# Earlier zeros for the experts' rows, later router loads and preparation, in a hybrid attention and mixture-of-experts block

## The chip, the cores and the metric

The kernel runs on one core of a Trainium2 chip. The metric is the device time of one launch in microseconds. Five engines run side by side, each through its own list of instructions in a fixed order: PE (matrix multiply; its weight load is PEld), DVE (vector), ACT (scalar functions), POOL (a second vector engine) and SP, which here only issues transfers. ACT and POOL can issue transfers too; all of them run on the core's 16 DMA engines.

## The reference

One block over 512 tokens of width 1024, in fp32, cut here to what the change meets:

```
proj   = x @ w_in                              # many column groups
y_a    = gated_deltanet(conv+silu of q, k, v, gates a, b, z)
y_b    = nsa_attention(q, compressed / selected / window keys, values)
merged = sigmoid(gate)*y_a + sigmoid(gate)*y_b
h1     = layer_norm(a*x  + merged @ w_out)
h2     = layer_norm(a*h1 + attention(h1 @ wq, mem @ wkv) @ xa_wo)   # over the memory
p      = softmax(h2 @ w_group + b_group);  group = top 1 of 4
e      = 2 best of the group's 8 experts by softmax(h2 @ w_expert + b_expert)
ffn    = sum over chosen experts of wt * (silu(h2@w_gate) * (h2@w_up)) @ w_down
out    = layer_norm(a*h2 + ffn)
```

The router's two products share one pass: `wr` holds both weight matrices (40 columns). The kernel takes them on rows that are not yet normalised, so that the scale `ln2_g` is multiplied into `wr` beforehand, and two sums over the rows (`ws2`, with `ln2_g` and `ln2_b`) correct the result afterwards.

## The kernel before

**Precision.** Each large product is three matmuls: every operand is split into a high part (a copy by ACT, rounded, L138) and a low part (source minus high, on DVE or POOL, L139), and `mm3` adds high*high, high*low and low*high (L211, L212, L213). `load_w` (L144) loads 256 columns of a weight matrix by SP, 1 MB, and splits them at once; so each block of weights passes SP, ACT, DVE or POOL, and then PE.

**Order.** One Python generator, `Weave`, writes the program. `dense` yields the projection blocks one after the other with the next block's weights loaded ahead; `W.until("k01")` writes all blocks up to a label, and `W.chain(gen, label)` writes a chain of dependent steps and fills between them with that many microseconds of projection blocks. A scheduler then places the instructions of each engine by its own estimate; `tc.issue_after` pins what is in it behind a place. Each engine then runs its list strictly in order. Big tiles come from 21 buffers (`B8`), tiles of 128x512 from a ring of six (`t512`).

**The start.** Blocks z3, k00, k01 come first. `token_gates` (L357 to L385) computes the gates' decay `gg` by a chain of small DVE operations (L359 to L375), then two matmuls over it (L377, L378), and exponentials on ACT (L382, L381, L385); `rotary_sines` follows (L286, L287 on ACT, L288 to L290 on POOL). Each key head passes ACT L421, three DVE steps L424, ACT L427 and DVE L428 (convolution and silu), then is transposed by PE (L217) and squared by ACT (L460) into `sst`. When all four heads' sums of squares are there, `gdn_inverse(0)` starts on DVE with L480, and goes through ACT L499 (decay, from PE L496 and L497), DVE L505, a forward substitution on DVE (L534 and L535, 15 steps) and L542 to L547 to the first small matmuls at PE L554.

**The middle.** After the sparse attention (`nsa`), `merged_T` k=7 transposes and splits the last piece of `merged`, the input of `w_out` (`dense_ln`, L941 adds the residual). Then come the attention over the memory (L1086 to L1116), `xa_wo` by `dense_ln`, whose first 256 columns (j = 0) run in blocks of 128 tokens t = 0 to 3, the router (`raw`, `after`, `route`) and the 32 experts, whose rows are added by indirect writes (L1310) into `ybuf`, 4 MB in DRAM, that must hold zeros before. `clear_ybuf` writes these zeros: POOL sets one 128x512 tile to zero, and one DMA writes it 16 times over. It is called when the first block of the memory's projections, x0, is reached, by `mem_load`, between the loads of x1's weights and of the memory.

**The router's tiles.** `wr` and `rb` (weights and biases) and `gb`, `gbp` (`ln2_g`, `ln2_b` in two layouts) come by eight small DMAs from the ACT queue (L1155 to L1166), and DVE makes `ws2` from them (L1168, L1171). `router_sums` (L1176 to L1178) adds `ws2` over the partitions with one matmul and copies it back.

Of the kernel before, what the change touches and what calls it, by code (L numbers as in the profile page):

```python
# [27 lines left out]
OP = mybir.AluOpType  # L28
AX = mybir.AxisListType
# [4 lines left out]
KD = D // 128  # L34
# [50 lines left out]
def body(tc, I, O, dbg=None):  # L85
    nc = tc.nc
    ctx = ExitStack()
    with ctx:
        _body(ctx, tc, nc, I, O, dbg or {})


def _body(ctx, tc, nc, I, O, dbg):
    V, A, T, G = nc.vector, nc.scalar, nc.tensor, nc.gpsimd
# [12 lines left out]
    def dump(name, ap):  # L106
        if name in dbg:
            nc.sync.dma_start(dbg[name], ap)
# [12 lines left out]
    def B8(shape, dt=FT):  # L121
        return big.tile(shape, dt, name="b8", bufs=NB8)

    def t512(shape, dt=FT):
        return wk.tile(shape, dt, name="t512", bufs=6)
# [8 lines left out]
    def load_rows(dst, src):  # L134
        nc.sync.dma_start(dst, src.rearrange("(t p) d -> p t d", p=128))
# [98 lines left out]
    def to_T(dh, dl, src, n_tok_tiles):  # L234

        for k in range(KD):
            p = ps.tile([128, 512], FT, name="tp")
            for t in range(n_tok_tiles):
                T.transpose(p[:, t * 128:(t + 1) * 128], src(t, k), ident)
            n = n_tok_tiles * 128  # L240
            split(dh[k // 4][:, k % 4, :n], dl[k // 4][:, k % 4, :n], p[:, :n])
# [22 lines left out]
    def before(engine):  # L264

        return [i for i in nc.cur_bb.bb.instructions if i.engine == engine][-1]
# [17 lines left out]
    def rotary_sines():  # L284
        with tc.issue_after(before(mybir.EngineType.Activation)):
            A.activation(ropec, ropes, AF.Sin, scale=0.5)  # L286
            A.activation(ropes, ropes, AF.Sin)  # L287
        G.tensor_scalar(ropes, ropes, sgn, None, op0=OP.mult)  # L288
        G.tensor_tensor(ropec, ropec, ropec, op=OP.mult)
        G.tensor_scalar(ropec, ropec, -2.0, 1.0, op0=OP.mult, op1=OP.add)  # L290
        dump("ropec", ropec)
        dump("ropes", ropes)
# [4 lines left out]
    p = ps.tile([128, 512], FT, name="tp")  # L297
# [13 lines left out]
    def proj_ch(hi, lo, c, out):  # L311
        for k in range(KD):
# [6 lines left out]
                                     ap=[[0, 128], [1, 128]]))  # L319
# [660 lines left out]
    def clear_ybuf(eng):  # L980
        z = t512([128, 512])
        G.memset(z, 0.0)
        eng.dma_start(ybuf.rearrange("(p a) (b c) -> p (a b) c", p=128, b=2), z[:, None, :].to_broadcast([128, 16, 512]))
# [2 lines left out]
    ME = {}  # L986

    def mem_load():
        clear_ybuf(nc.sync)
        memh, meml = B8([128, KD, M], FR), B8([128, KD, M], FR)  # L990
        mn = B8([128, 2, D])
        load_rows(mn, I["mem"][0])
        to_T([memh[:, 0:4], memh[:, 4:8]], [meml[:, 0:4], meml[:, 4:8]],
             lambda t, k: mn[:, t, k * 128:(k + 1) * 128], 2)
        ME.update(h=memh, l=meml, k=B8([128, KD, M]), v=B8([128, 2, D]))

    def mem_block(j):
        def emit(hi, lo):
            if not ME:
                mem_load()  # L1000
            memh, meml = ME["h"], ME["l"]
            if j < 4:
                for c in range(2):
                    p = ps.tile([128, 512], FT, name="mm")
                    for k in range(KD):
                        yield 0.33
                        mm3(p[:, :M], hi[:, k, c * 128:(c + 1) * 128], lo[:, k, c * 128:(c + 1) * 128],
                            memh[:, k], meml[:, k], first=k == 0, last=k == KD - 1)
                    A.activation(ME["k"][:, 2 * j + c], p[:, :M], AF.Copy)
            else:  # L1010
                for t in range(2):
                    p = ps.tile([128, 512], FT, name="mm")
                    for k in range(KD):
                        yield 0.33
                        mm3(p[:, :256], memh[:, k, t * 128:(t + 1) * 128], meml[:, k, t * 128:(t + 1) * 128],
                            hi[:, k, :256], lo[:, k, :256], first=k == 0, last=k == KD - 1)
                    A.activation(ME["v"][:, t, 256 * (j - 4):256 * (j - 4) + 256], p[:, :256], AF.Copy)
        return ("x%d" % j, I["xa_wkv"][0], 256 * j, 256, emit)
# [25 lines left out]
    W.until("z3")  # L1044
    token_gates()
    rotary_sines()
    W.until("k01")
    W.chain(gdn_inverse(0), "k11")
    W.until("v01")
# [50 lines left out]
    for t in range(NT):  # L1100
        P = PP[t][:, 0].rearrange("p (a b) -> p a b", a=4)
        PT = PP[t][:, 1].rearrange("p (a b) -> p a b", a=8)
        for q in range(2):
            p = ps.tile([128, 512], FT, name="tp")
# [4 lines left out]
    for t in range(NT):  # L1109
        PT = PP[t][:, 1].rearrange("p (a b) -> p a b", a=8)  # L1110
        for q in range(2):
            po = ps.tile([128, 4, 128], FT, name="ga", bufs=4)
            for i in range(4):
                c = 4 * q + i
# [24 lines left out]
    def load_next(n):  # L1139
        for e, q in use[:n]:  # L1140
            WT[e, q] = load_gu(e, q) if q < 2 else load_down(e)
        del use[:n]

    early.close()
    late = ctx.enter_context(tc.tile_pool(name="late", bufs=1))
    identr = late.tile([128, 128], FR, name="identr")
# [5 lines left out]
    wr = late.tile([128, KD, 40], FT, name="wr")  # L1152
    wb = t512([128, KD, 40])
    V.memset(wr[:, :, 4:8], 0.0)
    nc.scalar.dma_start(wr[:, :, 0:4], I["moe_w_group"][0].rearrange("(k p) c -> p k c", p=128))  # L1155
    nc.scalar.dma_start(wr[:, :, 8:40], I["moe_w_expert"][0].rearrange("(k p) c -> p k c", p=128))
    rb = late.tile([128, 40], FT, name="rb")
    V.memset(rb[:, 4:8], NEG)
    for n, c0, c1 in (("moe_b_group", 0, 4), ("moe_b_expert", 8, 40)):
        nc.scalar.dma_start(rb[:, c0:c1], bass.AP(tensor=I[n].tensor, offset=I[n].offset, ap=[[0, 128], [1, c1 - c0]]))  # L1160

    gb = late.tile([128, 2, KD], FT, name="gb")
    gbp = late.tile([128, 2, KD], FT, name="gbp")
    for i, n in enumerate(("ln2_g", "ln2_b")):
        nc.scalar.dma_start(gb[:, i], I[n][0].rearrange("(k p) -> p k", p=128))
        nc.scalar.dma_start(gbp[:, i], I[n][0].rearrange("(p k) -> p k", k=KD))  # L1166
    for i, w_ in ((1, wb), (0, wr)):
        V.tensor_tensor(w_, wr, gb[:, i, :, None].to_broadcast([128, KD, 40]), op=OP.mult)  # L1168
    ws2 = late.tile([128, 2, 40], FT, name="ws2")
    for i, w_ in enumerate((wr, wb)):  # L1170
        V.tensor_reduce(ws2[:, i], w_.rearrange("p k c -> p c k"), axis=AX.X, op=OP.add)  # L1171

    def router_sums():
        p = ps.tile([128, 512], FT, name="tp")
# [425 lines left out]
    with tc.If(most > CAP):  # L1600
# [5 lines left out]
        for t in range(NT):  # L1606
            for q in range(2):
                p = ps.tile([128, 512], FT, name="tp")
# [54 lines left out]
```

## Time and profile before

| | us |
|---|---|
| median of 3 runs | 1255.44 (1253.97 to 1255.5) |
| profiled execution | 1254.66 |
| its span | 1252.9 |
| PE busy | 1161.7 (93%) |
| DVE busy | 658.2 (53%) |
| ACT busy | 459.3 (37%) |
| POOL busy | 181.9 (15%) |
| mean granted clock of PE | 0.969 |

The profile's times are microseconds from the start of the span. In a timeline a row gives the start, the duration, engine, line, operation, output<-input, and in brackets how long the engine had been idle and what released it. [...]

### The profile page before, as it was taken

What the parts mean: (1) busy time and instruction counts of PE and PEld (TensorE: products, weight loads), DVE (VectorE), ACT (ScalarE), POOL (GpSimd) and SP (SyncE); (2) the same over time, 40 slices, a digit from 0 to 9 for tenths busy, and PEclk for the clock granted to TensorE, in tenths of its full rate; (3) what the DMA queues carried; (4) which work ended last, traced back from release to release, by engine and by line L of the source; (5) the groups of instructions that cost most, each with busy time, mean ns of one, the idle gap of its engine ahead of it and who ended that gap; (6) DMA issues with size and microseconds to landing.
All of it is one profiled execution on the core that took longest, in us unless ns stands there. A gap on an engine that the chain in (4) does not pass through costs nothing. (4 is left out here: it accounts for less than half of the span.)

```text
span 1252.9 us, 20776 instructions
## 1 busy us (share of the span) xinstructions
PE 1161.7 (93%) x8356; PEld 925.4 (74%) x8356; DVE 658.2 (53%) x1657; ACT 459.3 (37%) x1093; POOL 181.9 (15%) x151
## 2 busy tenths in 40 slices
PE   6996998879999999999899899999989999999994
PEld 6885787758888879999798799789985455455532
DVE  4695477874775724556457758233484111111147
ACT  4643454534544214343345524334142111111224
POOL 4151221221000000000001102000020000000185
PEclk9998999989999999999899999999998999999997
DMA  8220212112142562212531343227546899999823
GB/s 268 68 68 3 68 34 69 34 35 69 39 131 69 173 212 69 69 35 67 187 93 58 122 120 101 68 67 255 204 145 248 302 384 380 407 392 379 338 77 133
DMA packets 101882, 189.22 MB, mean 151 GB/s; under 512 B 10246, under 2 KB 74438, under 8 KB 97680
## 3 DMA queue, kind: packets, MB, share of 16 engines
q1 hardware_dynamic: 93456, 181.58, 41.1%
q0 software_dynamic: 2224, 3.94, 1.0%
q10 hardware_dynamic: 6096, 2.27, 0.8%
q8 instruction: 68, 1.11, 0.4%
q14 instruction: 38, 0.31, 0.1%
HBM read 177.93 MB, written 13.63 MB: 153 GB/s over the span
## 5 line engine op out<-in xcount | busy, mean ns | idle before, releaser
L211 PE MATMUL mm<-b,b 128*128 128x256 f32 (+3 forms) x1216 | 404.2, 333 | 21.7 <-ACT b L138 7.2
L212 PE MATMUL mm<-b,b 128*128 128x256 f32 (+3 forms) x1216 | 392.2, 323 | 2.2 <-DVE b L139 2.2
L213 PE MATMUL mm<-b,b 128*128 128x256 f32 (+3 forms) x1216 | 391.5, 322 | 0.7 <-POOL b L139 0.4
L211 PEld LDWEIGHTS mm<-b,b 128*128 128x128 f32 x1216 | 233.1, 192 | 43.3 <-issue 17.1
L213 PEld LDWEIGHTS mm<-b,b 128*128 128x128 f32 x1216 | 233.1, 192 | 22.1 <-issue 3.8
L212 PEld LDWEIGHTS mm<-b,b 128*128 128x128 f32 x1216 | 233.7, 192 | 18.2 <-DVE b L139 2.8
L1447 PE MATMUL ga<-b,b 128*64 128x512 f32 x512 | 131.5, 608 | 6.8 <-DVE b L1334 6.8
L139 DVE TENSOR_TENSOR b<-b,b 128x2048 fp32r<-128x2048 f32 (+4 forms) x48 | 101.8, 2123 | 56.5 <-ACT b L138 48.0
L138 ACT ACTIVATE b<-b 128x2048 fp32r<-128x2048 f32 (+4 forms) x58 | 104.3, 1799 | 26.9 <-DMA b<-in_w_in_dram 7.4
L1447 PEld LDWEIGHTS ga<-b,b 128*64 128x64 f32 x512 | 38.4, 138 | 73.8 <-issue 64.1
L424 DVE SCALAR_TENSOR_TENSOR t<-mm,cw,t 128x511 f32<-128x511 f32 (+2 forms) x72 | 53.8, 747 | 32.3 <-ACT t L421 31.1
L217 PE MATMUL tp<-cs,b 128*128 128x128 f32 x376 | 59.4, 287 | 9.7 <-DMA cs<-in_cst_dram 5.9
L1462 PE MATMUL ga<-b,t 128*64 128x512 f32 x256 | 63.9, 593 | 0.5 <-ACT t L1306 0.5
L139 POOL TENSOR_TENSOR b<-b,b 128x2048 fp32r<-128x2048 f32 x10 | 45.9, 4593 | 123.2 <-ACT b L138 102.1
L1327 PE MATMUL mm<-t,b 128*128 128x256 f32 x240 | 61.5, 294 | 0.0
L1299 DVE SCALAR_TENSOR_TENSOR t<-t,ga 128x256 f32<-128x256 f32 x16 | 6.7, 420 | 98.2 <-ACT t L1298 98.1
L217 PEld LDWEIGHTS tp<-cs,b 128*128 128x128 f32 x376 | 45.4, 147 | 15.3 <-DMA cs<-in_cst_dram 5.9
L1327 PEld LDWEIGHTS mm<-t,b 128*128 128x128 f32 x240 | 48.8, 203 | 0.8 <-issue 0.8
L1462 PEld LDWEIGHTS ga<-b,t 128*64 128x64 f32 x256 | 20.0, 137 | 36.2 <-issue 35.1
L815 POOL MEMSET b<- 128x97 f32 x32 | 5.6, 179 | 272.6 <-PE ga L762 170.7
L1310 POOL DMA_INDIRECT ybuf<-b,idx x14 | 13.7, 980 | 215.4 <-ACT b L1470 111.2
L1306 ACT ACTIVATE t<-tp 128x256 f32<-128x256 f32 x16 | 6.1, 383 | 88.8 <-PE tp L217 88.8
(442 smaller groups left out, 1842.4 us busy)
## 6 DMA issues: line engine op xcount, KB each, us to landing
b<-in_moe_w_gate_dram SPq DMA_DIRECT2D x64, 512.0 KB, 10.3
b<-in_moe_w_up_dram SPq DMA_DIRECT2D x64, 512.0 KB, 10.7
b<-in_moe_w_down_dram SPq DMA_DIRECT2D x32, 1024.0 KB, 12.6
b<-in_w_in_dram SPq DMA_DIRECT2D x22, 1024.0 KB, 5.3
b<-in_w_in_dram SPq DMA_DIRECT2D x10, 1040.0 KB, 5.2
b<-in_cmp_w_dram SPq DMA_DIRECT2D x16, 512.0 KB, 8.4
b<-in_xa_wkv_dram SPq DMA_DIRECT2D x8, 1024.0 KB, 5.3
ybuf<-t SPq DMA_DIRECT2D x1, 4096.0 KB
```

The source lines that it names most:

```text
L138: A.activation(hi, src, AF.Copy)
L139: eng.tensor_tensor(lo, src, hi.bitcast(FT), op=OP.subtract)
L211: T.matmul(out, wh, xh, start=first, stop=False)
L212: T.matmul(out, wh, xl, start=False, stop=False)
L213: T.matmul(out, wl, xh, start=False, stop=last)
L217: T.transpose(dst_psum[:, i * 128:(i + 1) * 128], s_, ident)
L424: V.scalar_tensor_tensor(acc[:, s_:], pp[:, :S - s_], cw[:, c_:c_ + 1], acc[:, s_:], op0=OP.mult, op1=OP.add)
L1299: V.scalar_tensor_tensor(th, th, 1.0, ph[:, :256], op0=OP.add, op1=OP.mult)
L1310: G.indirect_dma_start(out=ybuf[:, :], out_offset=bass.IndirectOffsetOnAxis(ap=idx, axis=0), in_=yt, in_offset=None, bounds_check=2 * S - ...
L1327: T.matmul(p, rows_of(hl)(t)[:, c], sv, start=False, stop=t == NT - 1)
L1447: T.matmul(ph[64 * i:64 * i + 64], xg[:, k, 128 * pp + 64 * i:128 * pp + 64 * i + 64], WT[2 * pr + i, k // 4][:, :, k % 4], start=k == 0, ...
L1462: T.matmul(py[64 * i:64 * i + 64], hT[:, k, 64 * i:64 * i + 64], WT[2 * pr + i, 2][:, k, 512 * n:512 * n + 512], start=k == 0, stop=k == 1)
```

## The change

The zeros are written right after `rotary_sines`, by the ACT queue, instead of in `mem_load` by SP. The router's eight DMAs go from the ACT queue to SP's, pinned behind the SP instructions that stood there when the attention over the memory was written; the four DVE operations that make `ws2` are pinned behind DVE's.

```
--- before.py
+++ after.py
@@ -986,7 +986,6 @@
     ME = {}
 
     def mem_load():
-        clear_ybuf(nc.sync)
         memh, meml = B8([128, KD, M], FR), B8([128, KD, M], FR)
         mn = B8([128, 2, D])
         load_rows(mn, I["mem"][0])
@@ -1044,6 +1043,7 @@
     W.until("z3")
     token_gates()
     rotary_sines()
+    clear_ybuf(nc.scalar)
     W.until("k01")
     W.chain(gdn_inverse(0), "k11")
     W.until("v01")
@@ -1141,6 +1141,7 @@
             WT[e, q] = load_gu(e, q) if q < 2 else load_down(e)
         del use[:n]
 
+    behind_attention = [before(e) for e in (mybir.EngineType.SP, mybir.EngineType.DVE)]
     early.close()
     late = ctx.enter_context(tc.tile_pool(name="late", bufs=1))
     identr = late.tile([128, 128], FR, name="identr")
@@ -1152,23 +1153,26 @@
     wr = late.tile([128, KD, 40], FT, name="wr")
     wb = t512([128, KD, 40])
     V.memset(wr[:, :, 4:8], 0.0)
-    nc.scalar.dma_start(wr[:, :, 0:4], I["moe_w_group"][0].rearrange("(k p) c -> p k c", p=128))
-    nc.scalar.dma_start(wr[:, :, 8:40], I["moe_w_expert"][0].rearrange("(k p) c -> p k c", p=128))
     rb = late.tile([128, 40], FT, name="rb")
     V.memset(rb[:, 4:8], NEG)
-    for n, c0, c1 in (("moe_b_group", 0, 4), ("moe_b_expert", 8, 40)):
-        nc.scalar.dma_start(rb[:, c0:c1], bass.AP(tensor=I[n].tensor, offset=I[n].offset, ap=[[0, 128], [1, c1 - c0]]))
 
     gb = late.tile([128, 2, KD], FT, name="gb")
     gbp = late.tile([128, 2, KD], FT, name="gbp")
-    for i, n in enumerate(("ln2_g", "ln2_b")):
-        nc.scalar.dma_start(gb[:, i], I[n][0].rearrange("(k p) -> p k", p=128))
-        nc.scalar.dma_start(gbp[:, i], I[n][0].rearrange("(p k) -> p k", k=KD))
-    for i, w_ in ((1, wb), (0, wr)):
-        V.tensor_tensor(w_, wr, gb[:, i, :, None].to_broadcast([128, KD, 40]), op=OP.mult)
     ws2 = late.tile([128, 2, 40], FT, name="ws2")
-    for i, w_ in enumerate((wr, wb)):
-        V.tensor_reduce(ws2[:, i], w_.rearrange("p k c -> p c k"), axis=AX.X, op=OP.add)
+    with tc.issue_after(behind_attention[0]):
+        for i, n in enumerate(("ln2_g", "ln2_b")):
+            nc.sync.dma_start(gb[:, i], I[n][0].rearrange("(k p) -> p k", p=128))
+        nc.sync.dma_start(wr[:, :, 0:4], I["moe_w_group"][0].rearrange("(k p) c -> p k c", p=128))
+        nc.sync.dma_start(wr[:, :, 8:40], I["moe_w_expert"][0].rearrange("(k p) c -> p k c", p=128))
+        for n, c0, c1 in (("moe_b_group", 0, 4), ("moe_b_expert", 8, 40)):
+            nc.sync.dma_start(rb[:, c0:c1], bass.AP(tensor=I[n].tensor, offset=I[n].offset, ap=[[0, 128], [1, c1 - c0]]))
+        for i, n in enumerate(("ln2_g", "ln2_b")):
+            nc.sync.dma_start(gbp[:, i], I[n][0].rearrange("(p k) -> p k", k=KD))
+    with tc.issue_after(behind_attention[1]):
+        for i, w_ in ((1, wb), (0, wr)):
+            V.tensor_tensor(w_, wr, gb[:, i, :, None].to_broadcast([128, KD, 40]), op=OP.mult)
+        for i, w_ in enumerate((wr, wb)):
+            V.tensor_reduce(ws2[:, i], w_.rearrange("p k c -> p c k"), axis=AX.X, op=OP.add)
 
     def router_sums():
         p = ps.tile([128, 512], FT, name="tp")
```

Since the scheduler places every instruction anew, the order also moves where the diff says nothing. Names as `t_455` are tiles; behind the new tile of the zeros their numbers are higher by three.

On DVE, at the start: `t_408` (after: `t_411`) and `t_455` (after: `t_458`) are the first and the second key head of k00; `gg` is the end of the gate chain. Before:

```order
L424 SCALAR_TENSOR_TENSOR t_408<-mm,cw,t_408 128x509
L371 TENSOR_TENSOR gp<-gp,gu 128x32
L372 TENSOR_SCALAR gp<-gp 128x32
L373 TENSOR_TENSOR gp<-gp,gs 128x32
L374 SCALAR_TENSOR_TENSOR gp<-gx,gp 128x32
L428 SCALAR_TENSOR_TENSOR b_381<-t_413,t_408 128x512
L375 SCALAR_TENSOR_TENSOR gg<-gp,ea 128x32
L379 COPY gcum<-tp 128x32
L380 TENSOR_SCALAR gcn<-tp 128x32
L383 TENSOR_SCALAR egn<-egc 128x32
L384 TENSOR_TENSOR ekd<-gcn,tp 128x32
L424 SCALAR_TENSOR_TENSOR t_455<-mm,cw,t_455 128x511
```

After:

```order
L424 SCALAR_TENSOR_TENSOR t_458<-mm,cw,t_458 128x510
L371 TENSOR_TENSOR gp<-gp,gu 128x32
L424 SCALAR_TENSOR_TENSOR t_458<-mm,cw,t_458 128x509
L372 TENSOR_SCALAR gp<-gp 128x32
L371 TENSOR_TENSOR gp<-gp,gu 128x32
L372 TENSOR_SCALAR gp<-gp 128x32
L371 TENSOR_TENSOR gp<-gp,gu 128x32
L428 SCALAR_TENSOR_TENSOR b_384<-t_463,t_458 128x512
L372 TENSOR_SCALAR gp<-gp 128x32
L373 TENSOR_TENSOR gp<-gp,gs 128x32
L374 SCALAR_TENSOR_TENSOR gp<-gx,gp 128x32
L375 SCALAR_TENSOR_TENSOR gg<-gp,ea 128x32
```

The gate chain's end, L375, stood ahead of the second head's three L424; now it stands behind them and behind that head's L428, which waits for ACT's L427.

On ACT, from there to the third key head's silu (`t_508` and `t_513`, after: `t_511` and `t_516`). Before:

```order
L421 ACTIVATE t_455<-mm,cw 128x512
L138 ACTIVATE b_479<-b_477 128x8x256
L427 ACT_TABLE_LOAD
L427 ACTIVATE t_460<-t_455 128x512
L421 ACTIVATE t_508<-mm,cw 128x512
L499 ACTIVATE b_599<-ga,gcn 128x128 x4
L458 ACTIVATE b_382<-tp 128x512
L460 ACTIVATE sq,sst<-tp 128x128 x4
L427 ACTIVATE t_513<-t_508 128x512
L421 ACTIVATE t_555<-mm,cw 128x512
```

After:

```order
L458 ACTIVATE b_385<-tp 128x512
L460 ACTIVATE sq,sst<-tp 128x128 x4
L138 ACTIVATE b_482<-b_480 128x8x256
L421 ACTIVATE t_511<-mm,cw 128x512
L499 ACT_TABLE_LOAD
L499 ACTIVATE b_602<-ga,gcn 128x128 x8
L427 ACTIVATE t_516<-t_511 128x512
L421 ACTIVATE t_558<-mm,cw 128x512
L458 ACTIVATE b_385<-tp 128x512
L460 ACTIVATE sq,sst<-tp 128x128 x4
L427 ACTIVATE t_563<-t_558 128x512
```

Eight of the L499, which wait for PE, now stand ahead of the third head's L427; four stood behind the third head's L421.

On ACT, at the last split of `merged` (`b_6847`) and the split of the second block of `w_out` (`b_7340`). Before:

```order
L138 ACTIVATE b_6847<-tp 128x512
L854 ACTIVATE sq<-mm,a_7260 128x128
L1155 DMA wr<-in_moe_w_group_dram 128x8x4
L1156 DMA wr<-in_moe_w_expert_dram 128x8x32
L1160 DMA rb<-in_moe_b_group_dram 128x4
L1160 DMA rb<-in_moe_b_expert_dram 128x32
L138 ACTIVATE b_6847<-tp 128x512
L138 ACTIVATE b_7340<-b_7338 128x8x256
```

After:

```order
L899 DMA b_7335<-in_ln_b_dram 128x1024
L138 ACTIVATE b_6847<-tp 128x512
L854 ACTIVATE sq<-mm,a_7260 128x128
L138 ACTIVATE b_6847<-tp 128x512
L138 ACTIVATE b_7340<-b_7338 128x8x256
L138 ACTIVATE b_7450<-b_7448 128x8x256
L138 ACTIVATE b_7560<-b_7558 128x8x256
```

The four DMA issues that stood between the two splits of `b_6847` are gone, and so are the four behind `b_7340`.

On ACT, at the first blocks of `xa_wo`: `b_8388` and `b_8389` are the splits of the attention's output, `b_8699` the split of the second 256 columns' weights, `ws` the router's sums. Before:

```order
L138 ACTIVATE b_8388<-ga 128x512 x2
L1177 ACTIVATE ws_8664<-tp 128x80
L1017 ACTIVATE b_6371<-mm 128x256 x2
L138 ACTIVATE b_8388<-ga 128x512 x2
L138 ACTIVATE b_8389<-ga 128x512 x4
L138 ACTIVATE b_8699<-b_8697 128x8x256
L138 ACTIVATE b_8809<-b_8807 128x8x256
```

After:

```order
L138 ACTIVATE b_8388<-ga 128x512 x2
L1016 ACTIVATE b_6371<-mm 128x256 x2
L138 ACTIVATE b_8388<-ga 128x512 x2
L138 ACTIVATE b_8389<-ga 128x512 x4
L1181 ACTIVATE ws_8654<-tp 128x80
L138 ACTIVATE b_8699<-b_8697 128x8x256
L138 ACTIVATE b_8809<-b_8807 128x8x256
```

The copy of the sums, L1177, stood ahead of the attention's last outputs; as L1181 it now stands directly ahead of the split of `b_8699`.

On PE, the matmul of the sums moves with it: the last rows of `xa_wo` j = 0 (weights `b_8384`) and the first of j = 1 (`b_8699`). Before:

```order
L213 MATMUL mm<-b_8384,b_8391 128x256
L211 MATMUL mm<-b_8384,b_8389 128x256
L212 MATMUL mm<-b_8385,b_8389 128x256
L213 MATMUL mm<-b_8384,b_8391 128x256
L217 MATMUL tp<-cs,b_7331 128x128 x2
L211 MATMUL mm<-b_8699,b_8388 128x256 x2
L212 MATMUL mm<-b_8700,b_8388 128x256
```
After:

```order
L211 MATMUL mm<-b_8384,b_8389 128x256
L212 MATMUL mm<-b_8385,b_8389 128x256
L213 MATMUL mm<-b_8384,b_8391 128x256
L1180 MATMUL tp<-ws_8654,ones 128x80
L217 MATMUL tp<-cs,b_7331 128x128 x2
L211 MATMUL mm<-b_8699,b_8388 128x256 x2
L212 MATMUL mm<-b_8700,b_8388 128x256
```

Before, that matmul (L1176) stood some 146 rows earlier, inside the attention's last products; now it stands behind the whole of j = 0.

## Rows read from the trace of the kernel before

**Rows 1.** The page, parts 1 and 5: busy time; out<-in xcount | busy, mean ns | idle before.
```profile
PE 1161.7 (93%) x8356; PEld 925.4 (74%) x8356; DVE 658.2 (53%) x1657; ACT 459.3 (37%) x1093; POOL 181.9 (15%) x151
...
L1447 PE MATMUL ga<-b,b 128*64 128x512 f32 x512 | 131.5, 608 | 6.8 <-DVE b L1334 6.8
```

**Rows 2.** Timeline of PE, 92 to 112 us: start, duration, line, [idle before <-releaser].
```profile
101.87 1.93 PE L554 MATMUL ga<-b 32*32 32x32 f32 x128 [9.01 <-DVE b L547]
```

**Rows 3.** Timeline of PE, 615 to 621 us.
```profile
620.66 0.55 PE L211 MATMUL mm<-b,b 128*128 128x252 f32 x1 [4.77 <-DVE sq L856]
```

**Rows 4.** Timeline of PE, 719 to 724 us.
```profile
719.84 0.33 PE L217 MATMUL tp<-cs,b 128*128 128x128 f32 x1
...
723.08 0.39 PE L211 MATMUL mm<-b,b 128*128 128x256 f32 x1 [2.08 <-ACT b L138]
```

**Rows 5.** Timeline of PE, 884 to 888 us.
```profile
884.39 0.38 PE L217 MATMUL tp<-cs,b 128*128 128x128 f32 x2
...
887.26 0.39 PE L212 MATMUL mm<-b,b 128*128 128x256 f32 x1 [1.82 <-DVE b L139]
```

**Rows 6.** Windows: length, busy us of each engine (instructions), PEclk, DMA share, GB/s.
```profile
620.00:625.00 5.00, 4.33 (x20) 4.37 (x21) 2.64 (x14) 1.57 (x7) 0.46 (x1) 0.50 1.06 411
724.00:728.00 4.00, 4.00 (x23) 4.00 (x22) 3.10 (x3) 1.89 (x2) 0.00 (x0) 0.57 1.08 207
888.00:892.00 4.00, 4.00 (x24) 4.00 (x23) 0.19 (x1) 0.00 (x0) 0.00 (x0) 0.57 0.79 259
```

**Rows 7.** Timeline of the SP queue, 609 to 640 us.
```profile
609.15 0.37 SPq L144 DMA_DIRECT2D b<-in_xa_wkv_dram  x1
609.57 0.62 SPq L983 DMA_DIRECT2D ybuf<-t  x1
```

**Rows 8.** Timeline of ACT, 609 to 618 us.
```profile
615.64 1.91 ACT L138 ACTIVATE b<-b 128x2048 fp32r<-128x2048 f32 x1 [5.37 <-DMA b<-in_xa_wkv_dram]
```

**Rows 9.** The page, part 6: DMA issues, KB each, us from issue to landing.
```profile
b<-in_xa_wkv_dram SPq DMA_DIRECT2D x8, 1024.0 KB, 5.3
```

**Rows 10.** Timeline of ACT with its queue, 717 to 723 us.
```profile
717.60 0.39 ACTq L1155 DMA_DIRECT2D wr<-in_moe_w_group_dram  x1
...
718.68 3.21 ACTq L1160 DMA_DIRECT2D rb<-in_moe_b_group_dram  x1
...
722.43 0.60 ACT L138 ACTIVATE b<-tp 128x512 fp32r<-128x512 f32 x1 [4.56 <-issue]
```

**Rows 11.** Waits of the SP queue, 800 to 860 us: total us, times, longest.
```profile
SPq L1123 <- PE mm L213: 20.1, 1, 20.1
```

**Rows 12.** Timeline of DVE, 728 to 732 us.
```profile
729.86 0.78 DVE L1171 TENSOR_REDUCE ws<-t 128x40 f32<-128x320 f32 x1
```

**Rows 13.** Timeline of DVE, 884 to 886 us.
```profile
884.92 2.28 DVE L139 TENSOR_TENSOR b<-b,b 128x2048 fp32r<-128x2048 f32 x1
```

**Rows 14.** Windows, as in rows 6.
```profile
28.00:44.00 16.00, 15.93 (x83) 13.22 (x82) 10.54 (x36) 6.24 (x13) 0.00 (x0) 1.00 0.03 5
41.70:62.70 21.00, 21.00 (x134) 18.64 (x133) 11.23 (x17) 17.87 (x58) 3.21 (x3) 1.00 0.33 101
62.70:101.80 39.10, 29.06 (x226) 27.35 (x224) 37.70 (x82) 14.11 (x32) 16.63 (x7) 0.93 0.17 54
```

**Rows 15.** Timeline of ACT, 33 to 62 us.
```profile
33.70 0.23 ACT L364 ACTIVATE gu<-gu 128x32 f32<-128x32 f32 x1 [2.61 <-DVE gu L363]
...
46.02 0.70 ACT L421 ACTIVATE t<-mm,cw 128x512 f32<-128x512 f32 x1
...
60.24 0.88 ACT L499 ACTIVATE b<-ga,gcn 128x128 f32<-128x128 f32 x3 [0.81 <-PE ga L497]
```

**Rows 16.** Timeline of DVE, 36 to 63 us.
```profile
40.56 0.18 DVE L375 SCALAR_TENSOR_TENSOR gg<-gp,ea 128x32 f32<-128x32 f32 x1
...
46.84 2.32 DVE L424 SCALAR_TENSOR_TENSOR t<-mm,cw,t 128x511 f32<-128x511 f32 x3 [4.57 <-ACT t L421]
...
62.67 0.18 DVE L480 TENSOR_SCALAR se<-sst 128x16 f32<-128x16 f32 x1 [2.52 <-ACT sq L460]
```

## The prediction

> **What bounds the kernel now.** I read the page's busy times first, then PE's waits, then each place that the change touches as timelines of all engines, and last the windows for the clock. PE is busy for 93% of the span [rows 1], so an edit counts only where PE stands still or runs at half speed, and the reader is to see four such places. At 101.87 us PE has waited 9.01 us for DVE's L547 [rows 2]: the forward substitution. At 620.66 it has waited 4.77 us for the split of x1's weights [rows 3]. At 723.08 it has waited 2.08 us for the last split of `merged` [rows 4]. At 887.26 it has waited 1.82 us for the weights of the second 256 columns of `xa_wo` [rows 5]. After the last three the clock stood at its lower level for some microseconds: 0.50, 0.57, 0.57 [rows 6]. In the experts' stage PE's waits before its largest group of products, 6.8 us in all, are for DVE's L1334 and none for a transfer [rows 1], so what is gained or lost before that stage is carried to the end.
>
> **Step A, the zeros leave 609 us: -1.2.** The load of x1's weights is issued at 609.15 and the 4 MB of zeros directly behind it [rows 7]; the split of these weights starts at 615.64, when the load has landed [rows 8], 6.5 us after its issue. Loads of this kind take 5.3 us in the median [rows 9]. Without the zeros on the same engines it should land 1.2 us earlier, and the ACT, DVE and PE steps behind it follow at once; PE would still wait 3.6 us. The gap's half clock (5 us at 0.50 [rows 6], worth 2.5 us) may shorten with it: bounds -0.5 (the two transfers hardly met) and -2.9 (1.2 and two thirds of that 2.5). I take -1.2, since a gap of 3.6 us is still longer than the 2.08 and 1.82 us after which the clock fell too [rows 4 to 6]. For the load of the memory, which is issued behind the zeros, I count nothing: PE's wait of this stretch is the one named.
>
> **Step B, the router's loads leave 717 us: -3.8.** Four DMA issues stand on ACT's queue from 717.60 on, the third of which takes 3.21 us; ACT's split of the last piece of `merged` has been held 4.56 us by them and starts at 722.43 [rows 10]. Its input, PE's transpose, is ready at 719.84 + 0.33 = 720.17 [rows 4]. Without the issues it starts at about 720.25, so the whole chain (split 0.60, DVE's L139, PE) comes 2.2 us earlier, and of PE's gap of 2.08 us next to nothing is left. The window 724 to 728 stands at 0.57 [rows 6], which costs 4 x 0.43 = 1.7; with no gap ahead of it I take it that this goes too. Sum 2.1 + 1.7 = 3.8; bounds -2.1 (the clock falls all the same) and -4.0. What is late next is PE's own list: it has matmuls of another block until the split is there.
>
> [...]
>
> On SP the eight issues now stand between the last load of the memory's weights and the first of the experts'. SP's wait for a buffer there is 20.1 us [rows 11], and the eight issues fit into it (two of 3.2 us and six of 0.6 at most would take 10). DVE's four operations for `ws2` (the longest 0.78 [rows 12], so 3 together at most) now run behind the attention's last split, ahead of the first L941 of `xa_wo`; that L941 has a spare PSUM tile behind it, so it may be a microsecond late at no cost; without that cover PE would wait for it as long as the L941 is late, 1 us.
>
> **Step C, the sums' copy ahead of a split: +2.5.** Before, ACT's split of the second 256 columns of `xa_wo` is long done when DVE's half, queued behind L941 of t = 3, runs from 884.92 for 2.28 us without any wait of its own [rows 13]; PE waits for it until 887.26 [rows 5]. Now ACT's copy L1181 stands ahead of that split, and it waits for PE's L1180, which stands behind the last matmul of j = 0, at 884.4 [rows 5]. Queued behind the copy are this split and two more. So: L1180 until 884.8, copy until 885.1, ACT's split (as long as the one of 1.91 [rows 8]) until 887.0, DVE 2.28 until 889.2, PE at 889.2 where it was 887.26: +2.0. PE's gap is then about 3.8 us, and a longer time at half clock follows a longer gap: 5 us at 0.50 after 4.77, 4 us at 0.57 after 1.82 [rows 3, 5, 6]. I add 0.5 for it; bounds +1.7 and +3.7 (another 4 us at 0.57).
>
> **Step D, the early zeros: +5.2.** The write itself is covered: from 28 to 44 us the DMA engines are almost idle (share 0.03 [rows 14]), at the 411 GB/s seen beside the old write [rows 6] 4 MB take 10 us, and ACT has 2.61 us to spare ahead of L364 [rows 15] for an issue of 0.62 [rows 7]. The price is in the order. `gg` ended at 40.56 [rows 16]. Now it stands behind the second head's L424 and L428: that head's matmuls end at about 40.8, L421 takes 0.70 [rows 15], the three L424 2.32 [rows 16], ACT's L427 some 0.6, L428 some 0.7 (over as many numbers as one L424, a third of 2.32), and then three small steps of the gate chain and `gg`, 0.2 each. That is 40.8 + 0.7 + 2.3 + 0.6 + 0.7 + 0.8 = 45.9, and with the hops between engines 46.7: 6.1 late, and ACT's exponentials of the gates with it, at 47.8 for 41.7. PE waits about 1.5 us for it, and makes that good later. From 41.7 to 62.7 ACT has 17.9 us of work [rows 14] and 3.1 idle, until the last square lets DVE's L480 start at 62.67 [rows 16]. Of that work the second head's copy and silu (1.2) now lie before it, and more of L499 stands ahead of the squares, twelve for seven (three take 0.88 [rows 15]: five more, +1.4). So the same work starts 6.1 late; of the idle time about 0.9 is made good, because PE is then further on: 6.1 - 1.2 + 1.4 - 0.9 = 5.4, and step by step through ACT's new list I come to 67.9 for L480, +5.2, which I take. From L480 to L547 DVE has no slack: 37.7 of 39.1 us busy [rows 14], so L547 and PE's L554 move by the same 5.2; PE's filling work ends some 92.9 us into the span (9.01 before 101.87 [rows 2]), and with its new waits near 98 at the latest, so that PE can't take it up. Bounds: +3.0, if all of ACT's 3.1 us of idle time went (6.1 - 3.1), and +6.5, if the second four L499 wait for PE as the three did at 60.24 [rows 15] and PE in turn for their PSUM tile, 1.3 more.
>
> **The sum**, against the profiled execution's 1254.66: -1.2 - 3.8 + 2.5 + 5.2 = +2.7, or 1257.4. The median of the runs stands 0.8 above that execution, so I forecast 1258.2 for the median, between 1256.3 and 1260.
>
> **The rivals.**
> 1. *The start takes it up.* The inverse's start doesn't rest on `gg`: the squares that release L480 need only the heads' convolutions, and two of those come earlier now. Then D is near 0 to +1, and the sum -1.2 - 3.8 + 2.5 + 0.5 = -2.0, with B and A at their better ends -4: 1251.5 to 1253.5, faster. For it: L460 needs no gate. Against it: L499 does, and in ACT's list eight of them stand ahead of the third head's L427. It decides from the point where L480 starts before 64 us.
> 2. *Half of it.* D at +3.0, or the clock's three low stretches shrink more than taken: +0.5, 1255.9, no change.
> 3. *More waits.* D at +6.5, C at +3.7, B at -2.1: -1.2 - 2.1 + 3.7 + 6.5 = +6.9, 1262; half of these mishaps give 1260.5.
> 4. *The change does not do what it says at 609 us*: the load of x1 takes its 6.5 us from other causes, and A is 0. That adds 1.2 to any of the others and is within the ranges.
>
> **How the numbers follow.** My forecast 0.50, the first rival 0.22, the second 0.16, the third 0.12 (the fourth lies within them). A change of under 0.2%, 2.5 us, can't be told from none here: faster is below 1252.9, slower above 1257.9. The first rival gives 0.15 of its 0.22 to faster, the second 0.04, my forecast 0.02 from better clock: 0.21. Above 1257.9 lie some 0.28 of my forecast's 0.50, since its middle is about there, and nearly all of the third: 0.41 with a little of the others. The rest is 0.38. The range for eight in ten leaves out a tenth at either end: 1251.8 to 1261.3.
>
> **What would show it.** Step D: `gg` at about 46.7, L480 at about 67.9 and L554 at about 107; L480 before 64 would make the forecast wrong. Step A: x1's weights split at 5.3 us from their issue, PE's wait near 3.6. Step B: the last `merged` split directly behind its transpose, no gap of PE there and PEclk 1.00 behind. Step C: PE's gap at `xa_wo` j = 1 of near 3.8 us, ACT's copy L1181 released by PE's L1180. Between these places the two profiles should run parallel; a difference in the experts' stage would be something that I have not seen.

## The result, and the profile after

The changed kernel took 1264.46 us in the median of 5 runs (1262.66 to 1264.84) beside 1255.5 for the kernel before; the ratio is 1.0052, with the 95% interval 1.0035 to 1.0069: slower by 4.4 to 8.7 us. The forecast was 1258.2, with a range of 1251.8 to 1261.3, so the sign was right and the time lay outside. The profiled execution took 1263.11 us (span 1261.3).

The page of the changed kernel, part 1 (the row of before is in [rows 1]); PE is "busy" for 6.5 us more with the same 8356 instructions:

```profile
PE 1168.2 (93%) x8356; PEld 930.4 (74%) x8356; DVE 659.9 (52%) x1657; ACT 459.2 (36%) x1093; POOL 181.4 (14%) x151
```

**The start.** DVE's timeline of the changed kernel, against [rows 16]. The last row is L547, which releases PE's L554:

```profile
48.00 0.19 DVE L375 SCALAR_TENSOR_TENSOR gg<-gp,ea 128x32 f32<-128x32 f32 x1
...
69.23 0.18 DVE L480 TENSOR_SCALAR se<-sst 128x16 f32<-128x16 f32 x1 [2.41 <-ACT sq L460]
...
107.40 0.68 DVE L547 TENSOR_TENSOR b<-t,cs 128x512 f32<-128x512 f32 x1
```

`gg` starts at 48.00 for 40.56, L480 at 69.23 for 62.67, L547 at 107.40 for 101.13. How much later an instruction starts than its like in the profile of before is called its lag below. 1.50 us of these lags belong to the execution: DVE's first L332, which runs ahead of the orders that changed, starts at 22.52 for 21.02 (and at 20.58 in a second profile of the same kernel, e0 below). ACT's timeline shows the chain as predicted:

```profile
42.94 0.69 ACT L421 ACTIVATE t<-mm,cw 128x512 f32<-128x512 f32 x1 [1.72 <-PE mm L213]
46.07 0.63 ACT L427 ACTIVATE t<-t 128x512 f32<-128x512 f32 x1 [2.44 <-DVE gp L372]
49.14 0.23 ACT L382 ACTIVATE egc<-gcum 128x32 f32<-128x32 f32 x1 [2.44 <-DVE gcum L379]
...
58.78 1.14 ACT L499 ACTIVATE b<-ga,gcn 128x128 f32<-128x128 f32 x4
60.26 1.14 ACT L499 ACTIVATE b<-ga,gcn 128x128 f32<-128x128 f32 x4 [0.33 <-PE ga L497]
```

The second head's L421 and L427 come first, the gates' L382 at 49.14, then eight L499, the second four released by PE's L497. PE's timeline, first its wait for `gg`, last the wait that stands against [rows 2]:

```profile
48.24 0.41 PE L377 MATMUL tp<-gg,cs 128*128 128x32 f32 x2 [1.18 <-DVE gg L375]
...
76.97 0.58 PE L211 MATMUL mm<-b,b 128*128 128x256 f32 x1 [4.15 <-ACT b L717]
...
108.14 1.07 PE L554 MATMUL ga<-b 32*32 32x32 f32 x64 [7.00 <-DVE b L547]
```

PE waits 1.18 us for `gg`, 4.15 for ACT's L717, and at 108.14 it has still waited 7.00 for L547, so that the whole delay of L547 passes to PE.

**What the forecast did not have** stands behind it. The windows of the kernel before and of the changed kernel around PE's small matmuls L560 and L564; in both PE is idle for over half of the first window. PEclk, the third figure from the end of a row, is the clock granted to PE in that stretch, as a share of full speed:

```profile
108.00:112.00 4.00, 1.78 (x164) 1.64 (x151) 1.75 (x3) 0.63 (x1) 0.00 (x0) 1.00 0.02 4
112.00:118.00 6.00, 6.00 (x107) 4.63 (x106) 1.82 (x2) 3.45 (x12) 0.00 (x0) 1.00 0.03 5
```

```profile
114.00:118.00 4.00, 1.77 (x170) 1.62 (x159) 2.07 (x3) 0.63 (x1) 0.00 (x0) 1.00 0.02 4
118.00:124.00 6.00, 6.00 (x82) 4.48 (x82) 1.82 (x2) 1.85 (x10) 0.00 (x0) 0.72 0.01 3
284.00:292.00 8.00, 6.04 (x212) 5.05 (x199) 2.50 (x3) 1.22 (x6) 0.00 (x0) 0.79 0.03 7
```

Before, the clock stays at 1.00 behind that gap; in the changed kernel it falls for part of the next 6 us (0.72; 0.50 from 120 to 122), and again behind the second inverse (0.79 from 284 to 292; 0.50 from 287 to 289). Such a stretch at 0.50 is called half clock here. DVE's L585 behind the first inverse is then 7.64 us late, and that behind the second 9.72.

**x1's weights.** SP's queue in the changed kernel, then ACT's split and PE's wait (against [rows 7], [rows 8], [rows 3]):

```profile
617.78 0.37 SPq L144 DMA_DIRECT2D b<-in_xa_wkv_dram  x1
627.42 0.37 SPq L135 DMA_DIRECT2D b<-in_mem_dram  x1
```

```profile
623.16 1.91 ACT L138 ACTIVATE b<-b 128x2048 fp32r<-128x2048 f32 x1 [4.26 <-DMA b<-in_xa_wkv_dram]
```

```profile
628.19 0.55 PE L211 MATMUL mm<-b,b 128*128 128x252 f32 x1 [3.66 <-DVE sq L856]
```

The load takes 5.4 us from issue to use for 6.5, and PE waits 3.66 us for 4.77.

**The last split of `merged`.** PE's transpose and ACT's split (against [rows 4], [rows 10]):

```profile
726.38 0.33 PE L217 MATMUL tp<-cs,b 128*128 128x128 f32 x1
```

```profile
726.74 0.60 ACT L138 ACTIVATE b<-tp 128x512 fp32r<-128x512 f32 x1 [2.34 <-PE tp L217]
```

```profile
720.00:728.00 8.00, 7.11 (x59) 6.50 (x58) 4.50 (x19) 2.43 (x5) 0.91 (x2) 1.00 1.03 360
728.00:732.00 4.00, 4.00 (x37) 4.00 (x36) 1.42 (x3) 1.92 (x1) 0.00 (x0) 1.00 1.10 348
```

The split starts 0.03 us behind its transpose's end; PE has no wait there, and PEclk stays at 1.00. Between the stage's two sides (L859 at 718.98 before, L924 at 754.79, from the timelines) the lag goes from 6.54 to 3.49: -3.05.

**The second 256 columns of `xa_wo`.** ACT, DVE and PE (against [rows 13], [rows 5]), and the window:

```profile
888.37 0.24 ACT L1181 ACTIVATE ws<-tp 128x80 f32<-128x80 f32 x1 [10.88 <-PE tp L1180]
```

```profile
890.43 2.29 DVE L139 TENSOR_TENSOR b<-b,b 128x2048 fp32r<-128x2048 f32 x1 [1.60 <-ACT b L138]
```

```profile
887.99 0.34 PE L1180 MATMUL tp<-ws,ones 128*128 128x80 f32 x2
...
890.45 0.68 PE L211 MATMUL mm<-b,b 128*128 128x256 f32 x2 [1.91 <-ACT b L138]
892.78 0.58 PE L212 MATMUL mm<-b,b 128*128 128x256 f32 x1 [1.65 <-DVE b L139]
```

```profile
892.00:896.00 4.00, 3.22 (x15) 3.22 (x16) 0.73 (x1) 2.01 (x2) 0.00 (x0) 0.50 0.50 162
```

ACT's copy waits 10.88 us for PE's L1180, the split follows it, DVE's half starts at 890.43, and PE waits 1.91 and then 1.65 us. The clock stands at 0.50 then. From L1106 to L1193 the lag grows from 3.61 to 6.10: +2.5.

SP's queue: all eight router loads are issued before the experts' first, though one, of 16 KB, took 2.76 us here. The load of 2 KB that held ACT's queue for 3.21 us [rows 10] took 0.68:

```profile
834.96 2.76 SPq L1165 DMA_DIRECT2D wr<-in_moe_w_group_dram  x1
...
838.39 0.68 SPq L1168 DMA_DIRECT2D rb<-in_moe_b_group_dram  x1
...
840.05 0.43 SPq L1170 DMA_DIRECT2D gbp<-in_ln_b_dram  x1
853.02 0.33 SPq L1123 DMA_DIRECT2D b<-in_moe_w_gate_dram  x1
```

### The profile page after: what moved, and what is told of

It is laid out like the page before. It is cut to its first block, busy times and chain, and to the rows that moved or that the text cites. A ratio compares the mean times of both kernels' runs of the same rounds, so it can differ in the third digit from the quotient of the medians.

```text
span 1261.3 us, 20782 instructions
## 1 busy us (share of the span) xinstructions
PE 1168.2 (93%) x8356; PEld 930.4 (74%) x8356; DVE 659.9 (52%) x1657; ACT 459.2 (36%) x1093; POOL 181.4 (14%) x151
## 3 DMA queue, kind: packets, MB, share of 16 engines
q8 instruction: 68, 1.11, 0.4%
## 5 line engine op out<-in xcount | busy, mean ns | idle before, releaser
L424 DVE SCALAR_TENSOR_TENSOR t<-mm,cw,t 128x511 f32<-128x511 f32 (+2 forms) x72 | 53.7, 746 | 32.9 <-ACT t L421 31.8
```

Of the source, the lines that this page charges most:

```text
L424: V.scalar_tensor_tensor(acc[:, s_:], pp[:, :S - s_], cw[:, c_:c_ + 1], acc[:, s_:], op0=OP.mult, op1=OP.add)
```

## The experiments

Each was timed in 5 rounds beside the kernel before on the same chip. The kernel before itself spreads: 75 runs on three chips lie between 1253.84 and 1262.41 us, with medians of 1257.52, 1257.28 and 1258.24. Differences below are the ratio and its 95% interval, times these medians.

**e0, the changed kernel again.** No edit.

> The changed kernel once more, on the chip of the other three. Theory S (the four steps are all there is): the start of the inverse (L480 less what the first loads bring) +5.1, x1 -1.8, the split of merged -3.0, the second columns of xa_wo +2.6, sum +2.9 us against the kernel before on the same chip; the other +4 us of the first profile (1.5 from the landing of the first loads, the rest from stretches at half clock at places that the change does not touch) belong to the execution and come out otherwise in this profile. Rival R (the rest belongs to the change): again +6 to +8.5 us, with half clock again at about 119 to 123 and 286 to 290 us.

Measured: 1.0055 (1.0033 to 1.0076), +6.9 us (4.1 to 9.6). L547 is 4.21 us late, L585 behind the first inverse 7.75, behind the second 9.49. The half clock is there again, at 115 to 122 and at 286 us (PEclk 0.92 from 60 to 300 us, as in the first profile; 0.95 before): theory S, that it was a matter of one execution, fell.

**e1, the zeros alone on ACT's queue.**

```
     def mem_load():
-        clear_ybuf(nc.sync)
...
     rotary_sines()
+    clear_ybuf(nc.scalar)
```

> Only the zeros are moved (same place and queue as in the change); the router's loads and preparation stay as before. Theory S: +5.1 - 1.8 = +3.3 us, L480 5 us later relative to the first matmul, nothing new at 717 and 885 us. Rival R: +6.5 us or more, since the shifted start brings further stretches at half clock with it. If the early order cost nothing: -1.8.

Measured: 1.0056 (1.0037 to 1.0074), +7.0 us (4.7 to 9.3). L480, from the timeline of its DVE:

```profile
68.41 0.17 DVE L480 TENSOR_SCALAR se<-sst 128x16 f32<-128x16 f32 x1 [2.41 <-ACT sq L460]
```

L480 is 5.74 us late, L547 5.41, L585 behind the second inverse 8.87. The whole of the slowdown is in this half of the change, and it is more than the steps.

**e2, the router alone.** The part of the diff from `behind_attention` on; the zeros as before.

> Only the router's loads and preparation are moved; the zeros stay in the memory's load. Theory S: -3.0 at the last split of merged and +2.6 at the second columns of xa_wo, sum -0.4 us, within 1 us of the kernel before. Rival (the eight small transfers delay the experts' first loads): +1 us or more, with PE waiting for a load behind 950 us.

Measured: 0.9995 (0.9981 to 1.0008), -0.6 us (-2.4 to +1.0). In its profile -3.35 at the split of `merged` and +2.52 at `xa_wo`, where PE waits twice:

```profile
884.36 0.61 PE L211 MATMUL mm<-b,b 128*128 128x256 f32 x2 [1.91 <-ACT b L138]
886.69 0.58 PE L212 MATMUL mm<-b,b 128*128 128x256 f32 x1 [1.72 <-DVE b L139]
```

At the end its lag is 0.0, and behind 950 us PE waits for no load: the experts' first loads weren't delayed. In between, from about 1013 to 1082 us, it is some 1.4 us, at most 2.4, ahead: the clock fell at 1011 in the profile of before and not in this one. The windows of before and of e2, with the same work of PE:

```profile
1010.00:1016.00 6.00, 4.86 (x22) 3.20 (x22) 1.52 (x7) 1.46 (x3) 0.96 (x1) 0.72 1.02 407
```

```profile
1010.00:1016.00 6.00, 4.86 (x35) 3.96 (x35) 2.44 (x8) 1.52 (x4) 0.97 (x1) 1.00 1.01 408
```

**e3, the zeros early but issued by POOL.** The edit of e1 with `nc.gpsimd` for `nc.scalar`; PE, ACT and DVE then keep the order of the kernel before at the start.

> The zeros are written at the same early place, but issued by POOL, in whose list they stand directly behind the zeroed tile; the order of PE, ACT and DVE up to the middle of the kernel is then that of the kernel before. The router is as before. Theory S (the price of the early zeros is the early order alone): the start is as before and x1 gains, -1.8 us. Rival W (the write itself holds up the start, by its traffic or its tile): +3 us or more, as with the zeros on ACT's queue.

Measured: 0.9993 (0.9975 to 1.0011), -0.9 us (-3.1 to +1.4). DVE's L480 and the split of x1's weights:

```profile
62.47 0.18 DVE L480 TENSOR_SCALAR se<-sst 128x16 f32<-128x16 f32 x1 [2.47 <-ACT sq L460]
```

```profile
613.86 1.91 ACT L138 ACTIVATE b<-b 128x2048 fp32r<-128x2048 f32 x1 [4.23 <-DMA b<-in_xa_wkv_dram]
```

L480 is where it was, and x1's split starts behind a wait of 4.23 us for 5.37: 1.14 gained. So the same 4 MB, written early, cost nothing; the price of e1 is the order, not the traffic. One thing differs: POOL issues the write at 21.92 us, ACT in e1 at 31.31, so the traffic isn't at the same time. But in e1 no engine waits for a transfer between 28 and 70 us.

**e4 (two kernels) and e7, a delay alone.** Identities on DVE in front of L542 of the first inverse, in the kernel before; every other engine keeps its order of compute instructions. `late_` is `tmp`, written across in the kernels marked t (n = 3, 4t, 5t). The expectations are, in this order, those of delay 3, of delay 5t, of delay 4t, of the zeros on ACT's queue once more, and of the kernel before once more.

```
+        if hf == 0:
+            for _ in range(n):
+                V.tensor_tensor(late_, yb, yb, op=OP.max)
+                V.tensor_tensor(yb, late_, late_, op=OP.max)
         for dst, v in ((XC, ...), (XTC, yb)):
```

> The same with six such operations, none written across: d = 2.2 to 2.6 us. Theory K: d plus up to 3, by which later gaps the clock still falls after; it needn't be in proportion to d. Rival N: d and no more.

> The kernel before, with ten DVE operations of 128x256 (identities on the substitution's result, five of them written across) in front of L542 of the first inverse; every engine's order is otherwise that of the kernel before, so that only L547 and PE's first small matmuls come later, by d = 4 to 6 us (read from the trace). Theory K (a later end of the substitution alone moves the later gaps so that the clock falls after other ones): d up to L547, then 1 to 3 us more up to the first L585 (half clock at about 115 to 122 us) and about 1.3 more behind the second inverse (half clock near 286), d + 3 in all. Rival N (the extra half clock needs the new early order, with its own stretch at 74 us): d and no more, half clock only where the kernel before has it.

> The kernel before, with eight identity operations on DVE in front of L542, 0.63 us each as the ten before it showed: L547 and PE's small matmuls come 5.1 us later, the shift that the early zeros gave, in the old order of every engine. Theory K (the shift is enough for all of it): +8 us, as the zeros alone on ACT's queue. Rival N (the early order has a price of its own behind the inverse): +5.1 us in the mean, with extra half clock only in some executions, as in those of the kernel before.

> The zeros alone on ACT's queue, as in the second experiment, beside the same shift in the old order on the same chip. Theory K: equal to the delay of 5.1 us less the 1.1 us of x1's load. Rival N: 2 us or more above it, and in the profile again half clock at 115 to 122, at 220 to 227 and at 286 us, which three of three profiles of the early order had and one of six of the old order without a delay.

> The kernel before itself, for its spread and a second profile: 0 against its own runs. If half clock at 115 to 122 and at 280 to 286 us comes and goes with the execution, a profile of an execution above 1257.5 us has it, and one at 1254 to 1255 does not.

Measured, beside the others; lags in us against the profile of before, from the timelines of DVE (L547 101.13, L585 121.71 and 288.14 there), and PEclk of the window 60 to 300 us (0.95 there):

| run | L547 | L585, first | L585, second | PEclk 60:300 | all runs |
|---|---|---|---|---|---|
| changed kernel | +6.27 | +7.64 | +9.72 | 0.92 | +6.5 (4.4 to 8.7) |
| e0, the same | +4.21 | +7.75 | +9.49 | 0.92 | +6.9 (4.1 to 9.6) |
| e1, zeros on ACT | +5.41 | +6.53 | +8.87 | 0.92 | +7.0 (4.7 to 9.3) |
| e7, zeros on ACT | +4.88 | +5.91 | +7.62 | 0.94 | +8.8 (5.7 to 12.1) |
| e4, delay 3 | +3.45 | +8.34 | +8.37 | 0.92 | +4.8 (2.0 to 7.5) |
| e7, delay 4t | +5.03 | +6.20 | +6.60 | 0.93 | +8.2 (5.2 to 11.1) |
| e4, delay 5t | +5.64 | +5.60 | +6.06 | 0.93 | +7.3 (3.8 to 10.8) |
| e2, router | -0.09 | -0.19 | -0.19 | 0.95 | -0.6 (-2.4 to 1.0) |
| e3, zeros on POOL | -0.19 | -0.53 | +0.07 | 0.94 | -0.9 (-3.1 to 1.4) |
| e6, router pinned | -0.61 | -1.15 | -1.27 | 0.95 | -2.8 (-4.5 to -1.0) |
| e5, both kept | -0.12 | +1.72 | +3.55 | 0.94 | -4.5 (-6.4 to -2.6) |
| e7, before again | +0.16 | +0.43 | +1.31 | 0.94 | +1.3 (-0.5 to 3.1) |

The delay of 4t is the nearest to the early order's: its L547 is 5.03 late, in an otherwise old order, and the kernel takes 8.2 us more; rival N's 5.1 lies 0.1 under the interval. Its PE wait and the windows behind it:

```profile
106.89 1.93 PE L559 MATMUL ga<-b 32*32 32x32 f32 x128 [14.03 <-DVE b L552]
```

```profile
112.00:116.00 4.00, 1.40 (x163) 1.30 (x151) 2.65 (x4) 0.63 (x1) 0.00 (x0) 1.00 0.01 4
116.00:120.00 4.00, 3.96 (x82) 3.20 (x82) 1.81 (x2) 1.28 (x9) 0.00 (x0) 0.61 0.01 4
284.00:288.00 4.00, 3.20 (x109) 2.55 (x109) 1.81 (x2) 0.23 (x1) 0.00 (x0) 1.00 0.01 4
```

The gap at 112 to 116 is followed by 0.61. The zeros again, on the same chip:

```profile
112.00:116.00 4.00, 1.65 (x191) 1.54 (x180) 2.58 (x4) 0.63 (x1) 0.00 (x0) 1.00 0.02 4
116.00:122.00 6.00, 6.00 (x104) 4.70 (x90) 1.81 (x2) 1.78 (x9) 0.00 (x0) 0.72 0.01 3
284.00:288.00 4.00, 3.42 (x106) 3.02 (x106) 1.79 (x2) 0.00 (x0) 0.00 (x0) 0.57 0.03 6
```

Theory K holds in kind: a delay alone, without any early order, makes the kernel slower, by more than the delay in the middle of each interval. That it is more than the delay is shown for 4t only, and barely. The delays put in are 2.7, 5.0 and 6.3 us (L547's lag less that of DVE's first L332, at 21 us); 2.7 and 6.3 lie within the intervals of 3 and 5t. As a statement on every profile theory K fell. 5t shows no half clock behind the gap at 112 to 116 (its low clock begins in the wait and ends at 112: 0.50 from 95 to 112, 0.99 from 112 to 124), while five of its 11 runs lie at 1269.5 to 1269.8, at a mean granted clock of 0.958 to 0.961, and the other six at 1257.1 to 1262.8, at 0.965 to 0.968. And e5, whose L547 is on time, has the same two stretches in its profiled execution:

```profile
112.00:116.00 4.00, 4.00 (x48) 3.11 (x49) 1.81 (x2) 1.77 (x9) 0.00 (x0) 0.63 0.01 4
278.00:284.00 6.00, 4.08 (x163) 3.52 (x150) 2.50 (x3) 0.55 (x5) 0.00 (x0) 0.72 0.02 5
```

So the gap behind the first inverse, 2.2 to 2.6 us of idle PE in the windows shown, is one after which the clock falls in some executions and not in others, and those in which the inverse ends later had it more often: 6 of 7 profiles against 1 of 6. What decides between the two no run shows; the two groups of 5t's runs, each with its own granted clock, show only that executions of the same instructions differ in it.

Behind the second inverse rival N's sign came: all four profiles of the early order have half clock there (0.79 and 0.57 in the two shown), none of the three delays (4t: 1.00) and one of the other six (e5). From the first L585 to the second the early order loses 1.7 to 2.3 us, the delays 0.0 to 0.5. In the time the zeros again are 0.6 us above 4t though x1 gives them 1.1, so 1.7 above theory K, where rival N asked for 2 or more; the intervals don't decide.

**A wait in the experts' stage** comes with the early order, too. DVE's L1397 adds the two parts of `h2` again, while POOL does so for other rows. Before, then e1:

```profile
1194.20 5.66 DVE L1397 TENSOR_TENSOR b<-b,hh 128x1024 f32<-128x1024 f32 x2
```

```profile
1206.35 7.64 DVE L1397 TENSOR_TENSOR b<-b,hh 128x1024 f32<-128x1024 f32 x2
```

```profile
1219.19 0.41 PE L217 MATMUL tp<-cs,t 128*128 128x128 f32 x2 [2.19 <-DVE t L1301]
```

The two operations take 7.64 us in all four profiles of the early order and 5.59 to 5.71 in the nine others, although the order of the lists is the same there (in the kernels with the router's edit the line is L1401 or L1402). DVE's L1301 stands behind them, and PE's transposes wait for it: 0.52 and 0.56 us in the two profiles of the changed kernel, 2.19 in e1 and in the zeros again, at most 0.26 elsewhere. From 1190 to 1230 us PE's lag grows by 2.3 us in three of these four, by 0.57 in e0, and in none of the others. Why the operations take longer is open; no run separates it.

**e6, the sums' copy put back behind the splits**, and **e5, both good parts.** e6 is e2 with

```
+        with tc.issue_after(before(mybir.EngineType.Activation)):
-        A.activation(ws2, pv, AF.Copy)
+            A.activation(ws2, pv, AF.Copy)
```

in `router_sums`; e5 is e6 with the zeros of e3.

> Only the router is moved, and ACT's copy of the router's sums is pinned behind the three splits of xa_wo's weights that it stood ahead of; the zeros stay in the memory's load. The gain at the last split of merged stays (-3.3 in the run with the router alone) and the loss at the second columns of xa_wo (+2.5 there) goes, if the copy's place is its cause: -3.3 us against the kernel before, PE's gap there back to 1.8 us. If the loss came from DVE's four operations behind the attention: still about -0.8.

> Both good parts: the router as in the run before this one, and the zeros early but issued by POOL, which leaves the order of the start alone. -3.3 of the router, and -0.6 to -1.1 of x1's load as in the run with the zeros on POOL: -4.1 us against the kernel before. If the zeros on POOL cost as much elsewhere as they bring: -3.3.

Measured: e6 0.9978 (0.9964 to 0.9992), e5 0.9964 (0.9949 to 0.9979), medians 1252.82 and 1252.71 for 1257.28. In e6 ACT's copy comes behind the splits, and PE's wait is the old 1.82 us; but the clock, which fell behind that wait before (0.57 [rows 6]), stays up:

```profile
881.23 1.91 ACT L138 ACTIVATE b<-b 128x2048 fp32r<-128x2048 f32 x1 [3.17 <-PE mm L212]
883.04 0.22 ACT L1182 ACTIVATE ws<-tp 128x80 f32<-128x80 f32 x1
```

```profile
884.02 0.38 PE L212 MATMUL mm<-b,b 128*128 128x256 f32 x1 [1.82 <-DVE b L139]
```

```profile
884.00:888.00 4.00, 3.98 (x33) 3.98 (x34) 0.92 (x2) 0.00 (x0) 0.00 (x0) 1.00 0.73 219
```

From L1106 to L1193 its lag goes from -3.25 to -4.77 where e2's went from -2.48 to +0.04. So e2's loss of 2.5 us came from the copy's place and not from DVE's four operations, which stand where they stood in e2; the other 1.5 us are the clock that stayed up in this execution, and in e5's, where it fell (the matmuls behind the same 1.82 us take 0.41 us for 0.28 ahead of it), the lag is the same on both sides (0.66 and 0.61). e5 and e6 can't be told apart; both are faster than the kernel before, by 0.4 and 0.2%.

## Why the prediction was right or wrong

**Step A (-1.2): right.** x1's wait at ACT fell by 1.11 us in the changed kernel and by 1.14 in e3, PE's by 1.11 and 1.13. How much of it stayed depended on the half clock behind that gap, in which PE worked for about 4.7 us before (620.7 to 625.4), 3.0 in the changed kernel (628.2 to 631.2) and 6.1 in e3 (618.9 to 625.0, with matmuls of 0.42 us for 0.28): DVE's lag from 600 to 660 us fell by 1.8 us in the changed kernel and by 0.6 in e3.

**Step B (-3.8): right in kind, 0.5 to 0.8 too large.** -3.05 and -3.35; the gap and the half clock behind it went, as said. The issues held ACT's split for 4.56 us [rows 10]; in the changed kernel, without them, it starts 0.03 us behind its input. That the third issue took long did not lie in its load alone: the load of 2 KB took 3.21 us on ACT and 0.68 on SP, that of 16 KB 0.39 on ACT and 2.76 on SP, and in both rows the long one was the third.

**Step C (+2.5): right.** +2.5 in the changed kernel and in e2, by the copy's place (e6). Its rule of thumb, a longer half clock after a longer gap, is no rule: behind the same 1.82 us the clock fell before (0.57) and not in e6 (1.00).

**Step D (+5.2): the chain and its size right, what follows from it wrong.** `gg` behind the second head, the eight L499, DVE without slack, PE with 7.00 us still to wait: each as written. The 0.8 us for the hops between engines was my estimate, from no row; in the changed kernel the three from the second head's L421 to its L428 took 0.03, 0.10 and 0.03 us. L547 was 4.21 to 6.27 us late in four profiles; less the lag that DVE's first L332 already has, it is 4.65 to 4.84 in each. What failed is the sentence of the first paragraph that what is lost before the experts' stage is carried to the end, by which the step's 5.2 us went into the sum one for one. It put at nothing what the clock does behind L547 and what the experts' stage does with the shift. The zeros alone cost 7.0 us (4.7 to 9.3) where 4.8 less x1's 1.1 would be 3.7, which lies under the interval. In place of the one for one the runs showed two things:

- Behind L547 come PE's groups of small matmuls with gaps between, after which the clock fell in 7 of the 13 profiles: the four profiles lose another 2.7 to 5.3 us by the second L585. The delays of e4 and e7 show that a later inverse can bring this on without a new order (their profiles lose 4.9, 1.6 and 0.4), though less of it behind the second inverse.
- In the experts' stage DVE's L1397 takes 2.0 us longer, and the lag grows by 0.6 to 2.3 us. This is the sign that the prediction named last, a difference in the experts' stage, and it came.

How the 3.3 us (1.0 to 5.6) above one for one divide between the two the medians don't tell. From e1, step D was worth about +8: its 7.0 and the 1.1 of x1's load, with 5.8 and 10.4 as the ends of the interval.

**The base.** I put the sum on one execution of 1254.66 and three runs of 1255.44. The median of 75 runs is 2 us above that. The longer executions of the kernel before are those at a lower clock: its 21 runs below 1256 us have a mean granted clock of 0.967 to 0.970, its ten from 1260 us on 0.962 to 0.966. Where the clock falls in them is open, since neither of its two profiles is of such a one (the second, of 1255.53 us, has no half clock at 113 to 122); the experts' stage is a candidate, as the windows at 1010 us show. Of the 6.3 us by which the forecast was short, the base is 2, step B 0.8, and most of the rest, nearly 4, what grew behind step D's shift.

**The rivals.** The first (the start takes it up) is excluded by L480 at 69.23, the second (half of D) by L547, 4.65 us late and more. The third, more waits, had the right size but other causes: C was not at +3.7 nor B at -2.1. The fourth is excluded by e3.

## What to carry to other kernels

A small edit can cost most through the order that a scheduler makes of everything around it: e3 shows the same early write for nothing, issued by POOL, which left the order of PE, DVE and ACT as it was. Where the clock behind PE's idle gaps falls in some executions and not in others (here in 7 of 13 profiles), one profile is one draw: look at PEclk over a long window in several executions before summing terms, and don't take a shift ahead of such gaps as carried one for one. Follow the lag to the last instruction: here part of the price came more than 1100 us behind the change. When work moves off a queue, look at what its result's consumers now stand in front of (here a copy of 0.24 us ahead of a split, for 2.5 us).

## What the runs showed of the hardware that I had not expected

One kernel on one chip (delay 5t) gave two groups of runs, 1257.1 to 1262.8 and 1269.5 to 1269.8 us, with every instruction the same; the mean granted clock was 0.965 to 0.968 in the first and 0.958 to 0.961 in the second. A small DMA's issue held its queue for 3.21 us (2 KB, on ACT) or 2.76 us (16 KB, on SP), and the same two loads took 0.68 and 0.39 us on the other queue. The same two DVE operations of 128x1024, beside POOL's, took 5.6 to 5.7 us in nine profiles and 7.64 in four.
